# The output projection, norm and first factors of token block 2 moved ahead of the last three chunks of token block 1's MLP

## The chip, the core and the metric

The kernel runs on one core of a Trainium2 chip. The metric is the device time of one execution in microseconds (us). PE (TensorE) multiplies matrices, DVE (VectorE) and ACT (ScalarE) work elementwise, POOL (GpSimd) and SP (SyncE) issue DMAs. Each engine works through its own instructions in the order in which they are written for it.

## The reference

It is one layer of an encoder on x with 2048 tokens of 1024 numbers, all in float32:

```python
h = rms_norm(x)                               # x (1, 2048, 1024)
z = h @ w_in                                  # q, k, v of 8 + 4 heads, gate
mix = concat(neighbourhood_attention(8 heads), bidirectional_retention(4 heads) * silu(gate))
y = x + mix @ w_out                           # "out projection"
h2 = rms_norm(y)
y = y + square(relu(h2 @ w_up)) @ w_down      # 1024 -> 4096 -> 1024
out = rms_norm(y)
```

## The kernel before, in words

Every float32 operand is split into a high and a low part, and a product is three matmuls, high x high, high x low and low x high (lines 191, 192, 193). The weights are streamed: SP loads a raw piece (L169), ACT rounds it to its high part `wh` (L181), DVE subtracts to get the low part `wl` (L182). The raw pieces have two buffers, the split ones four.

The tokens are four blocks of 512. Blocks 0 and 1 go through their MLP as plain products in `mlp(j)`. Its 4096 hidden columns are eight pieces; "u" is a piece of the up product with its squared ReLU and "d" a piece of the down product, which adds to y. A u chunk is 96 matmuls in eight steps. A d chunk is too, in two halves of the columns with 48 matmuls each. "o" is the output projection of one block, 192 matmuls in sixteen steps, in two halves as well. A table, WORK, lists the chunks of each block in order. Blocks 2 and 3 have their MLP done together afterwards, by a scheme with seven products of sums of quarters ("the last phase", from about 1800 us). It reads its first factors from the DRAM tensor d_s.

A chain `main` yields 512 steps: 0 to 191 input projection, 192 to 207 output projection of block 0, 208 to 351 `mlp(0)`, 352 to 511 `mlp(1)`. `interleave` runs other generators beside it, each given a number of its own steps and the first and last step of `main` between which they are spread. So attention, `na(j)`, and retention, `ret(j)`, of one block run beside the MLP of an earlier one. PE's order is the order in which this is written. The other engines' orders come from a scheduler that goes by priority; once set, they too are worked through in order.

The steps that the change moves:

- `mix_load(j)`: loads the attention's output of block j (SP, L1032, into the two raw buffers of the weight stream) and splits it on ACT and DVE (L1033, L1034).
- `out_proj(j)`, "o2" and "o3": matmuls whose evictions on DVE add the residual x (L1055), which SP loads into tiles `st` (L1044); POOL stores the sum to d_y (L1056); ACT sums its squares (L1022).
- `norm_in(j)`: for four tiles of 128 rows, SP loads the row tile from d_y into one of two `xn` buffers (L1088), DVE scales it (L1089), PE transposes it in two groups of four (`hp`, L1071), DVE scales by the gain (L1073), and POOL stores to d_hT (L1075).
- `prep_first_half`: eight "puts". SP loads a piece of d_hT into an `st` tile (L1112), ACT casts it (L1106), DVE subtracts (L1107), and SP stores the pair `so` into d_s (L1108). The tiles `so` are two in all, used alternately.
- `finish_block(0)`: the final norm of block 0 and its store (L1011, L1012).
- `lend`: gives the tiles of retention to the pool of `st`. `gain_halves`: a small preparation of the gain.

The squared ReLU of a u chunk is L951 to L954 (ACT, DVE, ACT, DVE), where L952 frees the PSUM bank and L954 writes the last piece that d reads. The eviction of a d chunk is L991 on DVE. Products of four PSUM banks run together, three matmuls to a bank in turn. There are five banks with the tag `mm`, so a group starts with one free bank and needs the others from the evictions of the group before. The line numbers before and after are the same up to the table, and one higher after it.

Of the kernel before, what the change touches and what calls it, by code (L numbers as in the profile page):

```python
# [77 lines left out]
def trunk(ctx: ExitStack, tc: tile.TileContext, x, xT, w_in, w_out, w_up, w_down, g_mix, g_mixT, g_mlp, g_mlpT, g_fin, g_ret,  # L78
# [35 lines left out]
    def nm(s):  # L114
        uid[0] += 1
        return f"{s}_{uid[0]}"

    def newton(v, n):

        yi = cp.tile([P, 4], I32, tag="nwi", bufs=2, name=nm("nwi"))[:, :n]  # L120
        dve.tensor_scalar(out=yi, in0=v.bitcast(I32), scalar1=-0.5, scalar2=-554214945.0, op0=ALU.mult, op1=ALU.add)
        y = cp.tile([P, 4], F32, tag="nwy", bufs=4, name=nm("nwy"))[:, :n]
        t = cp.tile([P, 4], F32, tag="nwt", bufs=2, name=nm("nwt"))[:, :n]
        cur = yi.bitcast(F32)
        for _ in range(3):
            if n == 1:
                dve.scalar_tensor_tensor(out=t, in0=cur, scalar=v, in1=cur, op0=ALU.mult, op1=ALU.mult)
            else:
                dve.tensor_tensor(out=t, in0=cur, in1=cur, op=ALU.mult)
                dve.tensor_tensor(out=t, in0=t, in1=v, op=ALU.mult)  # L130
            dve.scalar_tensor_tensor(out=y, in0=t, scalar=-1.5, in1=cur, op0=ALU.add, op1=ALU.mult)
            cur = y
        return y

    def half_stat(v, ss, rest=EPS / 2):

        if isinstance(rest, float):
            dve.tensor_scalar(out=v, in0=ss, scalar1=0.5 / D, scalar2=rest, op0=ALU.mult, op1=ALU.add)
        else:
            dve.scalar_tensor_tensor(out=v, in0=ss, scalar=0.5 / D, in1=rest, op0=ALU.mult, op1=ALU.add)  # L140
        return v

    def stat_tile(n):
        return cp.tile([P, 4], F32, tag="nwv", bufs=2, name=nm("nwv"))[:, :n]
# [90 lines left out]
    gml = {}  # L235
# [60 lines left out]
    def transpose_split(xn, t, hT):  # L296
        for q in range(2):
            ps = ax.tile([P, 4, P], F32, tag="ax", name=nm("hp"))
            for i in range(4):
                pe.transpose(ps[:, i], xn[:, (q * 4 + i) * P:(q * 4 + i + 1) * P], ident)  # L300
            hi, lo = hT
            sl = (slice(None), slice(q * 4, q * 4 + 4), slice(t * P, (t + 1) * P))
            act.copy(out=hi[sl], in_=ps)
            dve.tensor_sub(out=lo[sl], in0=ps, in1=hi[sl].bitcast(F32))

    def big_tile(i, dtype, shape):
        return big.tile(shape, dtype, tag=f"big{i}", name=nm(f"big{i}"))

    def pair(i):
        return (big_tile(2 * i, F32R, [P, KT, GT]), big_tile(2 * i + 1, F32R, [P, KT, GT]))  # L310

    def xtile():
        return cp.tile([P, D], F32, tag="xn", bufs=2, name=nm("xn"))
# [566 lines left out]
    def norm_rows(g):  # L880
        ss = cp.tile([P, 4], F32, tag="ss4", bufs=2, name=nm("ss"))
        for t in range(4):
            jk = xtile()
            act.activation(out=jk, in_=g.y[:, t], func=AF.Square, accum_out=ss[:, t:t + 1])
        return rms_stat(ss, 4)

    def norm_block(g, gain):
        r = norm_rows(g)
        xs = {}

        def scaled(t):
            if t < 4:
                xs[t] = xtile()
                dve.scalar_tensor_tensor(out=xs[t], in0=g.y[:, t], scalar=r[:, t:t + 1], in1=gain, op0=ALU.mult,
                                         op1=ALU.mult)

        yield
        scaled(0)
        scaled(1)
        yield  # L900
        yield
        g.hT = pair(0)
        for t in range(4):
            transpose_split(xs[t], t, g.hT)
            scaled(t + 2)
            yield
# [96 lines left out]
    def finish_block(g):  # L1003
        r = norm_rows(g)
        yield
        gf = xtile()
        sp.dma_start(out=gf, in_=g_fin)
        yield
        for t in range(4):
            yt = g.y[:, t]  # L1010
            dve.scalar_tensor_tensor(out=yt, in0=yt, scalar=r[:, t:t + 1], in1=gf, op0=ALU.mult, op1=ALU.mult)  # L1011
            st_dma.dma_start(out=out[g.j * GT + t * P:g.j * GT + (t + 1) * P, :], in_=yt)  # L1012
            yield
# [10 lines left out]
    def mix_load(j, mix):  # L1024

        for q in range(4):
            if q % 2 == 0:
                mix.append(big_tile(3 - q // 2, F32R, [P, 4, 2, GT]))
            m = mix[-1]
            ks = slice(2 * (q % 2), 2 * (q % 2) + 2)  # L1030
            t = wp.tile([P, 2, 512], F32, tag="raw", bufs=RAW, name=nm("mraw"))
            sp.dma_start(out=t, in_=d_mix[q * 256:(q + 1) * 256, j * GT:(j + 1) * GT].rearrange("(k p) t -> p k t", p=P))  # L1032
            act.copy(out=m[:, ks, 0], in_=t)  # L1033
            dve.tensor_sub(out=m[:, ks, 1], in0=t, in1=m[:, ks, 0].bitcast(F32))  # L1034
            yield
# [30 lines left out]
    def norm_tile(j, t, rows, new):  # L1066

        for q in range(2):
            ps = ax.tile([P, 4, P], F32, tag="ax", name=nm("hp"))
            for i in range(4):  # L1070
                pe.transpose(ps[:, i], rows[:, (q * 4 + i) * P:(q * 4 + i + 1) * P], ident)  # L1071
            e = new([P, 4, P])
            dve.tensor_tensor(out=e, in0=ps, in1=gmlpT[:, q * 4:q * 4 + 4].unsqueeze(2).to_broadcast([P, 4, P]),  # L1073
                              op=ALU.mult)
            st_dma.dma_start(out=d_hT[q * 512:q * 512 + 512, (j - 2) * GT + t * P:(j - 2) * GT + (t + 1) * P]  # L1075
                         .rearrange("(i p) t -> p i t", p=P), in_=e)

    def norm_in(j):

        h = half_stat(stat_tile(4), ssums[j, 0])  # L1080
        r = cp.tile([P, 4], F32, tag="rs4", bufs=4, name=nm("rs"))
        dve.tensor_copy(r, newton(half_stat(stat_tile(4), ssums[j, 1], h), 4))
        ys = {}

        def scaled(t):
            if t < 4:
                ys[t] = xtile()
                sp.dma_start(out=ys[t], in_=d_y[j * GT + t * P:j * GT + (t + 1) * P, :])  # L1088
                dve.tensor_scalar(out=ys[t], in0=ys[t], scalar1=r[:, t:t + 1], scalar2=None, op0=ALU.mult)  # L1089

        scaled(0)
        scaled(1)
        yield
        for t in range(4):
            norm_tile(j, t, ys[t], st)
            scaled(t + 2)
            yield
# [73 lines left out]
    for kind, _ in CHUNKS:  # L1171
        for q in range(4):
            ws.add(w_in, q * 256, COL[kind])
    WORK = [("u", 0)]
    for b in range(1, 7):
        WORK += [("u", b), ("d", b - 1)]
    WORK = [WORK + [("d", 6)] + outs + [("u", 7), ("d", 7)] for outs in ([("o", 1)], [("o", 2), ("o", 3)])]

    def add_out(j):
        idx["o", j] = len(ws.aps)  # L1180
# [5 lines left out]
    for j in range(2):  # L1186
        for kind, b in WORK[j]:
            if kind == "o":
# [326 lines left out]
    def late(fn):  # L1515
        yield from fn()

    with tc.manual_schedule(engines={mybir.EngineType.PE}):
# [33 lines left out]
        def lend(tags):  # L1552
            lent.extend("r_" + t for t in tags)
            yield

        def mlp(j):
            for kind, b in WORK[j]:
                if kind == "o" and b == 1:
                    yield from out_block(groups[1], idx["o", 1])
                elif kind == "o":  # L1560
                    yield from out_proj(b, mixes[b], idx["o", b])
                elif kind == "u":
                    yield from mlp_up(groups[j], b, idx["u", j, b])
                else:
                    yield from mlp_down(groups[j], b, idx["d", j, b])
# [5 lines left out]
        def unlend(tags):  # L1571
            for t in tags:
# [3 lines left out]
        groups = [Group(j) for j in range(2)]  # L1576
        mixes = {2: [], 3: []}
        main = chain(project(hTs, before), late(lambda: first_out_proj(groups[0], idx["o", 0], gml[0])),
                     late(lambda: mlp(0)), late(lambda: mlp(1)))
        ALL = ("qk", "v", "g", "st", "qx", "kT", "qxT", "a")  # L1580
# [9 lines left out]
                (late(lambda: mix_block(groups[0])), 4, 183, 190),  # L1590
                (na(1), NA_STEPS, 182, 270), (ret(1), RET_STEPS, 190, 262),
                (late(lambda: y_load(groups[1])), 1, 303, 303), (late(lambda: mix_block(groups[1])), 4, 311, 316),
                (late(lambda: norm_block(groups[1], gml[0])), 7, 337, 351), (late(lambda: finish_block(groups[0])), 6, 430, 450),
                (na(2), NA_STEPS, 271, 360), (ret(2), RET_STEPS, 263, 330),
                (na(3), NA_STEPS, 361, 452), (ret(3), RET_STEPS, 368, 430),
                (late(lambda: lend(ALL)), 1, 453, 453),
                (mix_load(2, mixes[2]), 4, 455, 460), (mix_load(3, mixes[3]), 4, 473, 479),
                (late(lambda: norm_in(2)), 5, 484, 490), (late(prep_first_half), 4, 491, 497),
                (late(lambda: norm_in(3)), 5, 500, 507), (late(gain_halves), 1, 500, 500)]
        interleave(main, fill)  # L1600
        first.close()

# [102 lines left out]
```

## Time and profile before

| | |
|---|---|
| runs, us | 2435.49, 2440.76, 2434.04; median 2435.49 |
| the profiled execution, us | 2439.59 |
| its span, us | 2437.8 |
| PE busy in the span | 2352.9 us, 97%, 11000 matmuls |
| DVE, ACT, POOL busy | 1543.8 (63%), 951.7 (39%), 242.8 (10%) us |
| DMA | 433.89 MB, mean 178 GB/s |
| granted TensorE clock, mean | 0.983 of full speed |

All views are of one profiled execution. Times of the trace count from the span's start. Busy time is the time in which an engine executes; the idle time before an instruction is set down to what released it last. An idle engine that is not the bottleneck costs nothing.

### The profile page before, as it was taken

Reading aid. Unit: us, or ns where it says so; the run is one execution under the profiler, and the core shown is the slowest. Engines: PE = TensorE matmul, PEld = TensorE weight load, DVE = VectorE, ACT = ScalarE, POOL = GpSimd, SP = SyncE. Lnnn points to the kernel's source line nnn. Section 1 sums busy time; section 2 is a strip of 40 time slices with the busy share of each in tenths; the row PEclk is TensorE's granted clock in tenths of the full one; section 3 lists DMA queues with packets and bytes.
Section 4 is the critical chain, followed back from the end, with each engine's and each line's share of the span. In section 5 each row is a group of like instructions: output and inputs, shape, how many; then the busy total and the mean of one; then the engine's idle time right before and its main releaser. Section 6 shows DMA issues by size and latency. Waiting matters only on the chain.

```text
span 2437.8 us, 31360 instructions
## 1 busy us (share of the span) xinstructions
PE 2352.9 (97%) x11000; PEld 1910.5 (78%) x11000; DVE 1543.8 (63%) x2996; ACT 951.7 (39%) x1656; POOL 242.8 (10%) x351
## 2 busy tenths in 40 slices
PE   7999999899999999999999999999889999999997
PEld 6788888677778777777877777878768888888885
DVE  7326364445467666667666667664569859668598
ACT  5313233222334334333444333333346436353364
POOL 1213022221100000000000000000110210000012
PEclk9999999999999999999999999999989999999999
DMA  8545565866656655556644555536887462443511
GB/s 274 184 139 174 169 210 185 260 217 188 200 159 169 168 158 147 158 169 186 171 124 146 152 150 169 172 123 223 289 316 292 147 241 96 173 173 104 215 61 70
DMA packets 238205, 433.89 MB, mean 178 GB/s; under 512 B 29792, under 2 KB 102112, under 8 KB 233824
## 3 DMA queue, kind: packets, MB, share of 16 engines
q1 hardware_dynamic: 200704, 291.07, 39.1%
q0 software_dynamic: 26512, 115.38, 13.3%
q10 hardware_dynamic: 10832, 25.44, 4.0%
q8 instruction: 88, 1.44, 0.2%
q14 instruction: 69, 0.57, 0.1%
HBM read 343.69 MB, written 88.08 MB: 177 GB/s over the span
## 4 chain that ended last, share of the span: by engine, by line
issue 32%; PE 30%; DVE 6%; POOL 2%; ACT 1%; DMA 1%; POOLq 0%; SPq 0%; DVEq 0%; ACTq 0%
PE mm L1250 5%; PE mm L1248 5%; PE mm L1249 5%; PE mm L191 4%; PE mm L193 4%; PE mm L192 4%; DVE narrow L1266 1%; DVE wide L1271 1%; DVE ff L1297 1%; PE tp L644 1%; PE op L661 1%; DVE y L1405 1%; PE sp L612 1%; POOL d_hT L1075 0%; POOL d_y L1056 0%
## 5 line engine op out<-in xcount | busy, mean ns | idle before, releaser
L191 PE MATMUL mm<-wh,big 128*128 128x512 f32 (+1 forms) x1272 | 506.2, 398 | 19.4 <-DVE st L427 8.7
L193 PE MATMUL mm<-wh,big 128*128 128x512 f32 (+1 forms) x1272 | 491.8, 387 | 3.5 <-DVE big L954 3.5
L192 PE MATMUL mm<-wl,big 128*128 128x512 f32 (+1 forms) x1272 | 489.6, 385 | 0.8 <-DVE wl L182 0.8
L1250 PE MATMUL mm<-wide,narrow 128*128 128x512 f32 x896 | 350.3, 391 | 6.5 <-DVE narrow L1266 6.5
L181 ACT CAST wh<-raw 128x1024 fp32r<-128x1024 f32 x208 | 218.2, 1049 | 353.4 <-PE mm L193 165.3
L1248 PE MATMUL mm<-wide,narrow 128*128 128x512 f32 x896 | 349.8, 390 | 3.8 <-ACT narrow L1265 3.2
L191 PE MATMUL mm<-big,wh 128*128 128x512 f32 (+1 forms) x864 | 345.1, 399 | 7.9 <-DVE st L1055 3.5
L1249 PE MATMUL mm<-wide,narrow 128*128 128x512 f32 x896 | 349.6, 390 | 0.0
L182 DVE TENSOR_TENSOR wl<-raw,wh 128x1024 fp32r<-128x1024 f32 x206 | 254.7, 1236 | 141.6 <-ACT wh L181 139.6
L193 PE MATMUL mm<-big,wl 128*128 128x512 f32 (+1 forms) x864 | 333.2, 386 | 0.0
L192 PE MATMUL mm<-big,wh 128*128 128x512 f32 (+1 forms) x864 | 332.4, 385 | 0.0
L191 PEld LDWEIGHTS mm<-wh,big 128*128 128x128 f32 x1272 | 243.8, 192 | 76.8 <-issue 11.1
L193 PEld LDWEIGHTS mm<-wh,big 128*128 128x128 f32 x1272 | 243.1, 191 | 52.5 <-DVE big L954 3.9
L192 PEld LDWEIGHTS mm<-wl,big 128*128 128x128 f32 x1272 | 244.1, 192 | 42.1 <-DVE wl L182 1.1
L1250 PEld LDWEIGHTS mm<-wide,narrow 128*128 128x128 f32 x896 | 168.8, 188 | 43.6 <-DVE narrow L1266 8.7
L191 PEld LDWEIGHTS mm<-big,wh 128*128 128x128 f32 x864 | 163.7, 189 | 46.8 <-issue 12.2
L1248 PEld LDWEIGHTS mm<-wide,narrow 128*128 128x128 f32 x896 | 168.9, 188 | 39.9 <-ACT narrow L1265 4.1
L1249 PEld LDWEIGHTS mm<-wide,narrow 128*128 128x128 f32 x896 | 168.7, 188 | 35.3
L620 ACT ACTIVATE ns<-ns,nsc 128x288 f32<-128x288 f32 (+3 forms) x128 | 79.2, 619 | 283.7 <-DVE nsc L615 184.7
L193 PEld LDWEIGHTS mm<-big,wl 128*128 128x128 f32 x864 | 163.3, 189 | 33.5
L192 PEld LDWEIGHTS mm<-big,wh 128*128 128x128 f32 x864 | 163.8, 190 | 26.4
L662 DVE TENSOR_REDUCE nt<-op 128x128 f32<-128x256 f32 x128 | 53.8, 421 | 145.0 <-PE op L661 144.7
(251 smaller groups left out, 2978.7 us busy)
## 6 DMA issues: line engine op xcount, KB each, us to landing
wide<-d_s POOLq DMA_DIRECT2D x21, 2048.0 KB, 8.2
raw<-in_w_up_dram SPq DMA_DIRECT2D x64, 512.0 KB
raw<-in_w_down_dram SPq DMA_DIRECT2D x64, 512.0 KB
raw<-in_w_in_dram SPq DMA_DIRECT2D x48, 512.0 KB
raw<-in_w_out_dram SPq DMA_DIRECT2D x32, 512.0 KB
wq<-in_w_up_dram SPq DMA_DIRECT2D x16, 1024.0 KB
wq<-in_w_down_dram SPq DMA_DIRECT2D x16, 1024.0 KB
nv<-d_v SPq DMA_DIRECT2D x288, 36.0 KB
```

The source lines that it names most:

```text
L181: act.copy(out=hi, in_=t)
L182: (eng or dve).tensor_sub(out=lo, in0=t, in1=hi.bitcast(F32))
L191: pe.matmul(bank, lhsT=sh, rhs=mh, start=first, stop=False)
L192: pe.matmul(bank, lhsT=sh, rhs=ml, start=False, stop=False)
L193: pe.matmul(bank, lhsT=sl, rhs=mh, start=False, stop=last)
L612: pe.matmul(s_ps, lhsT=ql[lo_, qs], rhs=k3[lo_, 0:rows, band:band + w], start=False, stop=True)
L620: act.activation(out=s, in_=s, func=AF.Exp, bias=sc[:, 0:1], scale=-1.0, accum_out=sc[:, 2:3])
L644: pe.transpose(t_ps[:, g], s[:, g * kk:(g + 1) * kk], ident)
L662: dve.tensor_reduce(out=t2[:, c], in_=o_ps.rearrange("p s q -> p q s"), axis=mybir.AxisListType.X, op=ALU.add)
L1248: pe.matmul(banks[m], lhsT=sh, rhs=mh, start=first_, stop=False, skip_group_check=True)
L1249: pe.matmul(banks[m], lhsT=sh, rhs=ml, start=False, stop=False, skip_group_check=True)
L1250: pe.matmul(banks[m], lhsT=sl, rhs=mh, start=False, stop=last_, skip_group_check=True)
```

## The change

The table of block 1 gets an order of its own: u0, u1, d0, u2, d1, u3, d2, u4, d3, then d4, o2, u5, u6, d5, d6, o3, u7, d7. Before, it was ..., d3, u5, d4, u6, d5, d6, o2, o3, u7, d7. The mix loads, the norm and the first factors of block 2, the loan of retention's tiles, the small preparation of the gain and the end of block 0 move to steps that suit. In steps of `main`: o2 goes from 464-479 to 432-447, norm_in(2) from 484-490 to 453-460, prep_first_half from 491-497 to 464-476, finish_block(0) from 430-450 to 370-390. o3, u7 and d7 keep their steps, 480 to 511.

```diff
@@ -1174,7 +1174,8 @@
     WORK = [("u", 0)]
     for b in range(1, 7):
         WORK += [("u", b), ("d", b - 1)]
-    WORK = [WORK + [("d", 6)] + outs + [("u", 7), ("d", 7)] for outs in ([("o", 1)], [("o", 2), ("o", 3)])]
+    early = WORK[:9] + [("d", 4), ("o", 2), ("u", 5), ("u", 6), ("d", 5), ("d", 6), ("o", 3), ("u", 7), ("d", 7)]
+    WORK = [WORK + [("d", 6), ("o", 1), ("u", 7), ("d", 7)], early]
 
     def add_out(j):
         idx["o", j] = len(ws.aps)
@@ -1590,13 +1591,13 @@
                 (late(lambda: mix_block(groups[0])), 4, 183, 190),
                 (na(1), NA_STEPS, 182, 270), (ret(1), RET_STEPS, 190, 262),
                 (late(lambda: y_load(groups[1])), 1, 303, 303), (late(lambda: mix_block(groups[1])), 4, 311, 316),
-                (late(lambda: norm_block(groups[1], gml[0])), 7, 337, 351), (late(lambda: finish_block(groups[0])), 6, 430, 450),
+                (late(lambda: norm_block(groups[1], gml[0])), 7, 337, 351), (late(lambda: finish_block(groups[0])), 6, 370, 390),
                 (na(2), NA_STEPS, 271, 360), (ret(2), RET_STEPS, 263, 330),
                 (na(3), NA_STEPS, 361, 452), (ret(3), RET_STEPS, 368, 430),
-                (late(lambda: lend(ALL)), 1, 453, 453),
-                (mix_load(2, mixes[2]), 4, 455, 460), (mix_load(3, mixes[3]), 4, 473, 479),
-                (late(lambda: norm_in(2)), 5, 484, 490), (late(prep_first_half), 4, 491, 497),
-                (late(lambda: norm_in(3)), 5, 500, 507), (late(gain_halves), 1, 500, 500)]
+                (late(lambda: lend(ALL)), 1, 431, 431),
+                (mix_load(2, mixes[2]), 4, 423, 430), (late(lambda: norm_in(2)), 5, 453, 460), (late(prep_first_half), 4, 464, 476),
+                (mix_load(3, mixes[3]), 4, 472, 479), (late(gain_halves), 1, 490, 490),
+                (late(lambda: norm_in(3)), 5, 500, 507)]
         interleave(main, fill)
         first.close()
 
```

The first place is DVE around the puts. Before, o3's evictions (L1055, adding to the residual) stand among the subtractions L1107 of the puts; L182 is the weight stream:

```order
L182 TENSOR_TENSOR wl_15527<-raw_15470,wh_15526 128x1024
L1107 TENSOR_TENSOR so_15502<-st_15500,so_15502 128x512
L1055 TENSOR_TENSOR st_15372<-mm_15380,st_15372 128x512
L1107 TENSOR_TENSOR so_15508<-st_15506,so_15508 128x512
L1055 TENSOR_TENSOR st_15374<-mm_15381,st_15374 128x512
L1055 TENSOR_TENSOR st_15376<-mm_15382,st_15376 128x512
L1055 TENSOR_TENSOR st_15378<-mm_15383,st_15378 128x512
```

After, the first two stand directly ahead of the squared ReLU of u6 (L952, L954):

```order
L182 TENSOR_TENSOR wl_14912<-raw_14863,wh_14911 128x1024
L1107 TENSOR_TENSOR so_14983<-st_14981,so_14983 128x512
L1107 TENSOR_TENSOR so_14989<-st_14987,so_14989 128x512
L952 TENSOR_TENSOR st_14930<-mm_14770,st_14930 128x512
L952 TENSOR_TENSOR st_14938<-mm_14771,st_14938 128x512
L954 TENSOR_TENSOR big_2894_14769<-st_14930,big_2894_14769 128x512
```

The third pair and the fourth stand around the evictions of d5 (L991):

```order
L991 TENSOR_TENSOR big_1858_9789<-mm_14967,big_1858_9789 128x512
L1107 TENSOR_TENSOR so_15105<-st_15103,so_15105 128x512
L991 TENSOR_TENSOR big_1858_9789<-mm_14968,big_1858_9789 128x512
L182 TENSOR_TENSOR wl_15042<-raw_15005,wh_15041 128x1024
L1107 TENSOR_TENSOR so_15111<-st_15109,so_15111 128x512
L1107 TENSOR_TENSOR so_15178<-st_15176,so_15178 128x512
L182 TENSOR_TENSOR wl_15088<-raw_15039,wh_15087 128x1024
L1107 TENSOR_TENSOR so_15184<-st_15182,so_15184 128x512
L991 TENSOR_TENSOR big_1858_9789<-mm_15057,big_1858_9789 128x512
```

The puts have moved from the evictions of o3 to those of u6 and d5.

The second place is SP's queue ahead of d7, the loads of norm_in(3). Before, stores of first factors stand between the loads `xn`:

```order
L1088 DMA xn_15697<-d_y 128x1024
L169 DMA raw_15660<-in_w_down_dram 128x2x512
L1108 DMA d_s_96<-so_15550 128x1024
L1108 DMA d_s_95<-so_15608 128x1024
L1088 DMA xn_15700<-d_y 128x1024
L1108 DMA d_s_96<-so_15614 128x1024
L169 DMA raw_15719<-in_w_down_dram 128x2x512
L1088 DMA xn_15741<-d_y 128x1024
```

After:

```order
L169 DMA raw_15599<-in_w_down_dram 128x2x512
L1088 DMA xn_15701<-d_y 128x1024
L169 DMA raw_15634<-in_w_down_dram 128x2x512
L1088 DMA xn_15704<-d_y 128x1024
L169 DMA raw_15664<-in_w_down_dram 128x2x512
L169 DMA raw_15719<-in_w_down_dram 128x2x512
L1088 DMA xn_15741<-d_y 128x1024
```

No store of a first factor is left among them.

## Rows read from the trace of the kernel before

**Rows 1.** Windows: start:end, length, each engine's busy time (instructions), PEclk, DMA share, GB/s

```profile
1110.00:1190.00 80.00, 79.92 (x381) 63.82 (x381) 53.33 (x112) 29.42 (x51) 2.63 (x4) 1.00 0.71 193
1231.00:1238.00 7.00, 7.00 (x21) 5.41 (x22) 3.27 (x6) 0.59 (x1) 0.00 (x0) 0.66 0.30 98
1440.00:1640.00 200.00, 199.29 (x930) 159.66 (x929) 129.40 (x268) 72.00 (x129) 7.16 (x12) 1.00 0.52 155
1640.00:1700.00 60.00, 58.17 (x256) 47.66 (x255) 30.79 (x44) 21.40 (x32) 4.37 (x8) 1.00 0.66 217
1720.00:1724.00 4.00, 4.00 (x13) 3.13 (x12) 2.43 (x5) 0.00 (x0) 2.65 (x4) 0.57 0.92 281
1742.00:1748.00 6.00, 5.67 (x14) 4.35 (x15) 4.53 (x7) 2.97 (x7) 2.19 (x4) 0.53 0.89 292
1760.00:1780.00 20.00, 15.74 (x70) 12.56 (x69) 13.37 (x20) 7.09 (x11) 3.53 (x4) 0.83 0.99 357
1773.00:1779.00 6.00, 5.99 (x19) 4.90 (x20) 6.00 (x10) 2.10 (x4) 1.01 (x1) 0.55 1.09 421
```

**Rows 2.** Waits of PE, 1636 to 1800: total us, times, longest us

```profile
PE mm L191 <- DVE st L1055: 5.7, 3, 3.5
PE mm L193 <- DVE big L954: 3.5, 1, 3.5
PE hp L1071 <- DVE st L1073: 1.0, 1, 1.0
PE mm L191 <- DVE big L991: 0.9, 1, 0.9
PE hp L1071 <- DVE xn L1089: 0.8, 1, 0.8
PE mm L191 <- ACT big L953: 0.8, 1, 0.8
```

**Rows 3.** Timeline, PE: start, length, line, tiles, count, [idle before <-releaser]

```profile
1230.99 1.01 PE L661 MATMUL op<-npt,nv 120*128 120x256 f32 x3 [4.80 <-DVE big L304]
...
1711.11 0.50 PE L191 MATMUL mm<-wh,big 128*128 128x512 f32 x1 [1.28 <-DVE st L1055]
...
1719.49 0.66 PE L1071 MATMUL hp<-ident,xn 128*128 128x128 f32 x4 [1.02 <-DVE st L1073]
...
1738.17 0.39 PE L192 MATMUL mm<-big,wh 128*128 128x512 f32 x1
1738.40 0.39 PE L193 MATMUL mm<-big,wl 128*128 128x512 f32 x1
1742.33 0.80 PE L191 MATMUL mm<-big,wh 128*128 128x512 f32 x1 [3.54 <-DVE st L1055]
```

**Rows 4.** Timeline, ACT, the first factors' casts

```profile
1731.59 0.62 ACT L1106 CAST so<-st 128x512 fp32r<-128x512 f32 x1 [3.23 <-DMA st<-d_hT]
1734.23 0.62 ACT L1106 CAST so<-st 128x512 fp32r<-128x512 f32 x1 [2.02 <-DMA st<-d_hT]
...
1740.33 0.62 ACT L1106 CAST so<-st 128x512 fp32r<-128x512 f32 x1 [4.53 <-DMA d_s<-so]
```

**Rows 5.** Timeline, DVE

```profile
1521.62 3.67 DVE L1011 SCALAR_TENSOR_TENSOR big<-big,nwy,xn 128x1024 f32<-128x1024 f32 x3
...
1694.20 0.75 DVE L1089 TENSOR_SCALAR xn<-xn,rs 128x1024 f32<-128x1024 f32 x1 [1.40 <-DMA xn<-d_y]
...
1740.98 0.69 DVE L1107 TENSOR_TENSOR so<-st,so 128x512 fp32r<-128x512 f32 x1 [3.92 <-ACT so L1106]
...
1771.01 0.75 DVE L1089 TENSOR_SCALAR xn<-xn,rs 128x1024 f32<-128x1024 f32 x1 [2.94 <-DMA xn<-d_y]
```

**Rows 6.** Timeline, SP's queue: issues of DMAs

```profile
1689.95 0.33 SPq L1088 DMA_DIRECT2D xn<-d_y  x1
...
1728.71 2.25 SPq L1112 DMA_DIRECT2D st<-d_hT  x5
...
1764.17 4.20 SPq L1088 DMA_DIRECT2D xn<-d_y  x2
```

## The prediction, made before the changed kernel ran

> **What bounds the kernel now.** The page comes first: PE, the TensorE matmul engine, is busy 97% of the span, so time is gained or lost only where PE stands still or runs at the lower clock. The change touches a stretch that ends at 1800 us, and a table of windows over it shows where PE is not full: attention with MLP chunks, 1440 to 1640, keeps it busy 199.29 of 200 us, while 1760 to 1780 reaches 15.74 of 20 at a granted clock of 0.83 [rows 1]. The list of PE's waits, cut to 1636 to 1800, names them: 5.7 + 3.5 + 1.0 + 0.9 + 0.8 + 0.8 = 12.7 us [rows 2]. The timeline places the large ones. Output projection o3 pauses between its halves (1.28) and around the last transposes of norm_in(2) (0.8, 1.02), and the first matmul of u7 waits 3.54 for an eviction of o3 [rows 2, 3]. The 3.5 on L954 is the first matmuls of d7, waiting for u7's squared ReLU.
>
> After the larger ones the clock falls from 2.4 to about 1.2 GHz. A window's length times what its granted clock lacks of 1 gives the cost: 4 x 0.43 = 1.7 after the transposes, 6 x 0.47 = 2.8 after the 3.54, 6 x 0.45 = 2.7 after the 3.51 [rows 1]. Idle time and clock together are 12.7 + 7.2 = 19.9 us, all that the change can win before 1800. What follows 1800 reads the same factors and is written in the same order, so I leave its waits alone.
>
> Two chains make the waits. The put of a first factor is a load of d_hT, a cast on ACT (L1106), a subtraction on DVE (L1107), and a store from one of two buffers. ACT stood 4.53 us for the stores d_s<-so of the first pair before it could cast again at 1740.33, and DVE stood 3.92 behind that cast [rows 4, 5]. DVE works in order, and o3's evictions (L1055) stand behind that subtraction: hence 3.54 on PE. At d7, DVE stands 2.94 us for a load xn<-d_y with u7's evictions behind it [rows 5].
>
> **The change, part by part.** Nothing is added or removed; every matmul, cast and DMA is issued once as before. What moves is o2, its mix loads, norm_in(2) with its two transposes per row tile and 4 stores, the 8 puts with 8 loads and 8 stores, and finish_block(0).
>
> What goes. Between o3's halves and at the transposes there is no norm_in(2) any more: 1.28 + 0.8 + 1.02 = 3.1, and the clock's 1.7: 4.8. At o3 to u7 no put stands among the evictions: 3.54 + 2.8 = 6.3. At u7 to d7 the load of xn is still ahead of the evictions on DVE, but eight d_s stores no longer share SP and the DMA engines with it. Issued at 1764.17, it let DVE start at 1771.01, 6.8 us later, at a DMA share of 0.99 [rows 1, 5, 6]. The like load issued at 1689.95 was used at 1694.20, 4.25 us later, at 0.66. So DVE is 2.6 us earlier; PE's 3.51 becomes 0.9, the 0.8 beside it stays, and I expect no fall of the clock after waits of that size (the 0.9 behind L991 and the 0.92 left of the 5.7 brought none; that stretch has a clock of 1.00 [rows 1, 2]). That saves 2.6 + 2.7 = 5.3. Bounds: nothing, if the load is no faster, and 6.7, if both waits shrink to 0.3. Together 4.8 + 6.3 + 5.3 = 16.4.
>
> A rule on this load, apart from that sum: the Trainium skill, "DMA: Bandwidth & Descriptors", section "Latency and other measured facts", gives an HBM access 0.2 us on average and 2 us at high load, and calls the fixed cost of a DMA smaller under lighter load. The trace agrees in sign, 6.8 against 4.25 us, but differs by 2.6 us and not by at most 1.8. By the page's figure, as an estimate, 0.8 us less would be won here, and the total would come out that much later.
>
> What comes back. (1) The puts now stand ahead of u6's squared ReLU: the first pair's cast on ACT and subtraction on DVE precede all four evictions. Before, the last transposes began at 1719.49 and ended 0.66 later, 1720.15; the first casts began at 1731.59 and 1734.23, 11.4 and 14.1 later, with the loads of d_hT issued at 1728.71, after the stores landed [rows 3, 4, 6]. In the new order 48 matmuls lie between those transposes and the end of u6, at 0.23 each [rows 3] 11.0 us, and d5 has one free PSUM bank, worth 3 matmuls or 0.7. If the second cast comes after 14.1, its subtraction and the first eviction (0.6 to 0.7 each) end at 16.1: PE waits 4.5. If it comes with the first cast, 11.4, the eviction ends by 13.4 and PE waits 1.7; with stores and loads each 0.5 faster than that, 0.7. I take 3.0, since the DMA share of that stretch should lie between 0.52 and 0.92 (attention's and the old place's [rows 1]); and 2.0 for the clock, between nothing and 2.8. Five together, 0.7 to 7.3.
>
> (2) d5 to d6. Puts stand among d5's evictions (L991) of one half and directly ahead of those of the other. With PE a whole half-chunk of matmuls (48, 11.0 us) behind each, the turnaround of a buffer pair, 1734.23 to 1740.33 or 6 us, mostly fits. I take 0.7, between nothing and 3.0 (the wait of 3.54 at u7, a little shorter).
>
> (3) o2 among attention. The mix loads and residual loads join the attention's loads on SP's queue, and PE is in order. The like combination ran in 1110 to 1190, the output projection of token block 1 beside na(2): 79.92 us busy of 80 [rows 1]. I take 0.5, between nothing and 3.0. What norm_in(2) costs there is in this too, as u5 and u6 run beside it.
>
> (4) o3 to u7 keeps an ordinary wait on an eviction like the others: 0.9 [rows 2]. finish_block(0), four DVE operations from 1521.62 [rows 5], goes from one attention stretch to another; it lay in 1440 to 1640, where PE lost 0.7 of 200, so nothing, at most 0.7. If attention's cover were gone, its four operations would cost 4 x 1.3 = 5 us of DVE.
>
> Sum: -16.4 + 5.0 + 0.7 + 0.5 + 0.9 = -9.3. The profiled execution took 2439.59, so 2430.3 in its place; it is 4.1 over the median of the runs, 2435.49, and a median should come to 2426.2.
>
> **Rivals.** (a) The puts' wait only changes its place. They are as long as before, and ACT and DVE still meet them in order ahead of evictions. Then u6 to d5 costs 7.3 and d5 to d6 the old 6.3: -9.3 + 2.3 + 5.6 = -1.4, 2434.1. For it: the same 4.53 for a store would stand ahead of L991. Against it: 11.0 us of matmuls in between.
>
> (b) The load of xn is no faster, because what it meets is the weight stream and the next phase's factors, which stay. u7 to d7 then keeps its 7.0: -9.3 + 5.3 = -4.0, 2431.5. For it: the 1.09 share of 1773 to 1779, when no put was left [rows 1]. Against it: the two stores issued shortly before.
>
> (c) Slower: SP's queue delays attention. A mix load waits for one of two weight buffers and a residual load for an st tile; loads of attention's values (nv) and of weights stand behind it. PE met a late attention product at 1230.99, idle 4.80, then 7 us at 0.66: 4.8 + 2.4 = 7.2 [rows 1, 3]. Two such waits leave +5.1, still within the noise; from the third it is slower: -9.3 + 21.6 = +12.3, 2447.8. For it: na(3) runs on through o2. Against it: 1110 to 1190.
>
> **How the numbers follow.** About 0.3%, 7.3 us, is what a measurement here can tell from no change: faster is under 2428.2, slower over 2442.8. The forecast has 0.60, with its own range from the best ends, -16.2 or 2419, to the worst of the sum's new terms, -4.7 or 2431; 0.50 of it is faster and 0.10 the same. A gain beyond 2419 has 0.04. Rival (a) has 0.14, all the same; (b) 0.11, of which 0.03 faster; (c) 0.11, slower. That makes 0.57, 0.32 and 0.11. The range from 2417 to 2438 holds the forecast, (a) and (b), and leaves out (c) and the largest gain.
>
> **What would show it.** In the profile after: no wait of PE between o3 and u7 above 1 us and no clock near 0.5 there; DVE's wait for xn before d7 well below 2.94; one new wait of 2 to 5 us at the start of d5, with ACT's casts L1106 released by st<-d_hT just before; no op L661 wait beside o2. I would be wrong if waits on L1055 or L991 of 3 us or more stand at d5 and d6 together, if d7's start still costs 3.5, or if PE has new waits on attention's products near o2.

## The result and the profile after

The changed kernel takes 2419.7 us (median of 4 runs, 2417.94 to 2423.2) against 2434.76 before: 15.1 us less, a ratio of 0.9933 with a 95% interval of 0.9921 to 0.9945. In five later rounds the ratio was 0.9932 (0.9913 to 0.9951). The forecast was faster, 2426.2 us in a range of 2417 to 2438. The time lies in the range and near its lower end: the gain is 1.6 times the 9.3 us that were worked out.

The page's span goes from 2437.8 to 2421.4 us. The windows after, to be held against [rows 1] (start:end, length, busy time of PE, PEld, DVE, ACT and POOL with their instructions, granted clock, DMA share, GB/s):

```profile
1440.00:1640.00 200.00, 199.31 (x946) 160.11 (x945) 128.19 (x269) 75.03 (x139) 15.76 (x24) 1.00 0.62 187
1640.00:1700.00 60.00, 58.22 (x255) 47.23 (x254) 36.31 (x47) 22.91 (x30) 0.00 (x0) 1.00 0.73 246
1700.00:1760.00 60.00, 60.00 (x276) 49.76 (x274) 29.17 (x45) 21.01 (x35) 5.87 (x10) 1.00 0.53 174
1760.00:1780.00 20.00, 18.39 (x89) 15.29 (x88) 8.18 (x14) 2.68 (x8) 7.15 (x10) 1.00 0.99 366
```

The clock is 1.00 in all of them, and the stretch after the puts, 1700 to 1760, has PE busy for 60.00 of 60 us at a DMA share of 0.53. The attention stretch with o2 and norm_in(2) in it, 1440 to 1640, loses 0.69 us, where it lost 0.71.

PE's waits up to the last phase, to be held against [rows 2]:

```profile
PE hp L1071 <- DVE st L1073: 1.6, 1, 1.6
PE mm L191 <- DVE st L952: 1.3, 2, 1.0
PE mm L191 <- DVE big L991: 0.5, 1, 0.5
```

They sum to 3.4 us, where they were 12.7. The timeline of PE gives their places (start, length, line, tiles, count, idle before), first the last transposes of norm_in(2) and the start of d5, then the transposes of norm_in(3) in d7 and the start of the last phase:

```profile
1631.76 1.04 PE L1071 MATMUL hp<-ident,xn 128*128 128x128 f32 x8
...
1645.36 0.50 PE L191 MATMUL mm<-wh,big 128*128 128x512 f32 x1 [0.99 <-DVE st L952]
...
1647.34 0.50 PE L191 MATMUL mm<-wh,big 128*128 128x512 f32 x1 [0.33 <-DVE st L952]
```

```profile
1761.74 0.66 PE L1071 MATMUL hp<-ident,xn 128*128 128x128 f32 x4 [1.61 <-DVE st L1073]
...
1784.40 0.50 PE L1249 MATMUL mm<-wide,narrow 128*128 128x512 f32 x1 [2.04 <-ACT narrow L1266]
```

The last phase began at 1801.01 before and begins at 1784.40, 16.6 us earlier. Idle time gives 12.7 - 3.4 = 9.3 of that, and the three half-clock stretches of [rows 1], all gone, give 7.2: 16.5. After that nothing has changed beyond 0.2 us.

Where the forecast put the new wait, at d5, 1.0 + 0.3 us stand without a fall of the clock. The casts of the first pair of puts on ACT, to be held against [rows 4]:

```profile
1639.50 0.62 ACT L1106 CAST so<-st 128x512 fp32r<-128x512 f32 x1 [0.35 <-DMA st<-d_hT]
1643.36 0.62 ACT L1106 CAST so<-st 128x512 fp32r<-128x512 f32 x1 [3.23 <-DMA st<-d_hT]
...
1656.41 0.62 ACT L1106 CAST so<-st 128x512 fp32r<-128x512 f32 x1 [4.28 <-DMA d_s<-so]
```

They come 6.7 and 10.6 us after the end of the transposes (1632.80), not 11.4 and 14.1. DVE's row at 1644.01, the subtraction of the second put, still stands directly ahead of the first evictions of u6, and the second row is the scaling of the third row tile ahead of d7, which waits for its load of xn, to be held against [rows 5]:

```profile
1644.01 0.69 DVE L1107 TENSOR_TENSOR so<-st,so 128x512 fp32r<-128x512 f32 x1 [2.99 <-ACT so L1106]
...
1754.22 0.75 DVE L1089 TENSOR_SCALAR xn<-xn,rs 128x1024 f32<-128x1024 f32 x1 [1.59 <-DMA xn<-d_y]
```

SP's issues of these loads, as [rows 6]:

```profile
1636.37 4.31 SPq L1112 DMA_DIRECT2D st<-d_hT  x6
...
1750.64 6.68 SPq L1088 DMA_DIRECT2D xn<-d_y  x2
```

The first load of d_hT goes out 3.6 us after the transposes, where it was 8.6; from its issue to the cast it takes 3.1 us, where it took 2.9. So the whole difference lies ahead of the load, and POOL's stores to d_hT show where, before and after:

```profile
1721.35 2.99 POOL L1075 DMA_DIRECT2D d_hT<-st  x4 [6.85 <-DVE st L1073]
```

```profile
1633.39 0.75 POOL L1075 DMA_DIRECT2D d_hT<-st  x1 [1.49 <-DVE st L1073]
1635.11 0.75 POOL L1075 DMA_DIRECT2D d_hT<-st  x1 [0.97 <-DVE st L1073]
```

After, the last two, of the fourth row tile, leave singly at 1633.39 and 1635.11, 0.6 and 2.3 us after the end of the transposes. Before, four of them left one behind the other from 1721.35, since DVE had stood 3.50 us for a load of xn (its scaling at 1716.95) with the evictions of two row tiles behind it. The first load of d_hT is issued when the first store of the fourth row tile has landed (1728.57 and 1728.71 before, 1636.31 and 1636.37 after). That store left 2.7 us after the transposes before and leaves 0.6 after; from its leaving to the load's issue it took 5.9 us and takes 3.0. The 5.0 us are thus 2.1 from DVE and POOL and 2.9 from the landing. That the new place is quieter does not show in the DMA share over the chain itself, before and after:

```profile
1720.00:1730.00 10.00, 10.00 (x39) 8.07 (x38) 3.66 (x6) 1.05 (x1) 2.99 (x4) 0.83 0.75 246
```

```profile
1636.00:1644.00 8.00, 8.00 (x37) 6.58 (x36) 1.83 (x2) 2.32 (x4) 0.00 (x0) 1.00 0.88 281
```

Over 1632 to 1636, as the last stores leave, it is 0.70. Further ahead the new place is the quieter one: 0.82 over 1620 to 1632, where it was 0.95 over 1705 to 1720.

The load of xn issued at 1750.64 is used at 1754.22, 3.6 us later, where it was 6.8. It also goes out earlier. Its buffer comes free when the first row tile of norm_in(3) has been transposed. These are those transposes before, with SP's last store of a first factor, and the transposes after:

```profile
1760.60 1.04 PE L1071 MATMUL hp<-ident,xn 128*128 128x128 f32 x8
```

```profile
1763.26 0.32 SPq L1108 DMA_DIRECT2D d_s<-so  x1
```

```profile
1749.57 1.04 PE L1071 MATMUL hp<-ident,xn 128*128 128x128 f32 x8
```

Before, the load (1764.17) stood in SP's order behind that store, which waited for the last put's subtraction, and went out 2.5 us after the buffer was free (1761.64). After, it goes out at once (1750.61 to 1750.64). From the free buffer to the scaling it is 3.6 us instead of 9.4.

### The profile page after: what moved, and what is told of

Read it like the earlier page. It is cut to its first block, busy times and chain, and to the rows that moved or that the text cites. A ratio compares the mean times of both kernels' runs of the same rounds, so it can differ in the third digit from the quotient of the medians.

```text
span 2421.4 us, 31361 instructions
## 1 busy us (share of the span) xinstructions
PE 2345.3 (97%) x11000; PEld 1906.1 (79%) x11000; DVE 1543.3 (64%) x2996; ACT 951.5 (39%) x1656; POOL 243.5 (10%) x351
## 4 chain that ended last, share of the span: by engine, by line
PE 36%; issue 26%; DVE 5%; DMA 1%; POOL 1%; ACT 1%; POOLq 0%; SPq 0%; DVEq 0%; ACTq 0%
PE mm L1251 6%; PE mm L1249 6%; PE mm L1250 6%; PE mm L191 5%; PE mm L193 5%; PE mm L192 5%; DVE narrow L1267 1%; DVE ff L1298 1%; PE tp L644 1%; PE sp L612 1%; DVE y L1406 1%; DVE wide L1272 1%; PE op L661 1%; DMA d_s<-so 0%; PE sp L610 0%
## 5 line engine op out<-in xcount | busy, mean ns | idle before, releaser
L182 DVE TENSOR_TENSOR wl<-raw,wh 128x1024 fp32r<-128x1024 f32 x206 | 254.6, 1236 | 137.0 <-ACT wh L181 134.5
```

The lines of the kernel that those rows point to most:

```text
L182: (eng or dve).tensor_sub(out=lo, in0=t, in1=hi.bitcast(F32))
```

## The experiments

Ratios are those to the kernel before on the same chip, with 95% intervals. Waits are of one profiled execution each. Single traces of one kernel differ by some us in parts that the change does not touch, so the ratio tells the time and the trace only the place. after_again came out as expected: 15.1 us under the kernel before, waits of 0.8 + 0.3 us at d5 and 1.7 at the transposes of norm_in(3), nothing ahead of u7.

| kernel | what is different | median us | ratio |
|---|---|---|---|
| after_again | nothing, the changed kernel | 2420.9 | 0.9932 (0.9913 to 0.9951) |
| puts_late | after, puts back | 2425.9 | 0.9944 (0.9926 to 0.9962) |
| norm_puts_late | after, norm_in(2) and puts back | 2432.3 | 0.9972 (0.9962 to 0.9982) |
| end0_late | after, end of block 0 back | 2420.1 | 0.9926 (0.9906 to 0.9945) |
| copies_norm2 | after, copies ahead of the puts | 2424.9 | 0.9954 (0.9936 to 0.9972) |
| copies_d7 | after, copies ahead of d7 | 2424.2 | 0.9940 (0.9922 to 0.9957) |
| so_five | before, five buffers so | 2438.7 | 1.0014 (1.0002 to 1.0026) |
| xn_behind | before, scaling of xn later | 2436.8 | 1.0003 (0.9992 to 1.0015) |
| norm2_480 | before, norm_in(2) four steps earlier | 2436.1 | 0.9994 (0.9984 to 1.0005) |
| norm2_early | after, puts four steps later | 2419.1 | 0.9937 (0.9919 to 0.9954) |
| norm2_449 | after, norm_in(2) four steps earlier | 2423.1 | 0.9937 (0.9922 to 0.9953) |
| norm2_norm3 | after, puts and norm_in(3) later | 2427.4 | 0.9963 (0.9950 to 0.9976) |

**The parts of the change undone.** First the puts alone:

```diff
-(late(prep_first_half), 4, 464, 476)
+(late(prep_first_half), 4, 491, 497)
```

> The changed kernel with prep_first_half alone back at steps 491 to 497. Theory: the waits at o3 to u7 and at u7 to d7 both came from the puts, so both return: about 3.5 us on L1055 ahead of u7 with a half-clock stretch, and 3 to 4 us on L954 or L953 ahead of d7 with another, the load xn<-d_y taking 6 to 7 us; the 1.3 + 0.5 at d5 and d6 goes. 2428 to 2433 us. Rival: the load of xn was slow because of norm_in(3)'s own order and not because of the puts: then only the wait ahead of u7 returns, 2424 to 2426 us.

PE's waits from 1636 to the last phase:

```profile
PE hp L1071 <- DVE st L1073: 1.7, 1, 1.7
PE mm L191 <- DVE st L1055: 0.9, 2, 0.6
```

Both theories miss. (The median lies in the rival's range, but the wait that the rival names is not there.) DVE's order is again a subtraction, an eviction of o3, a subtraction and three evictions, but the wait ahead of u7 is 0.9 us and nothing waits ahead of d7. What differs from the kernel before is that d_hT has been complete for long. Casts on ACT ahead of and among o3's evictions (the first row is two):

```profile
1722.74 1.37 ACT L1106 CAST so<-st 128x512 fp32r<-128x512 f32 x2 [3.00 <-DMA st<-d_hT]
...
1729.19 0.62 ACT L1106 CAST so<-st 128x512 fp32r<-128x512 f32 x1 [0.62 <-DMA d_s<-so]
```

The first put of all was cast at 1650.35; five follow from 1713.64 to 1729.19, around the evictions, and the last two at 1739.75 and 1740.77, in u7. The place of the puts in the queues of ACT and DVE is therefore not by itself what cost 3.54 us before. The third load of norm_in(3) goes out as soon as its buffer is free here too, at 1747.35. The ratio, 0.9944 against 0.9932, is not told from the changed kernel's, as the intervals overlap. In this trace the last phase begins at 1781.40; it then waits 3.4 us for its first factors.

Then norm_in(2) as well:

```diff
-(late(lambda: norm_in(2)), 5, 453, 460), (late(prep_first_half), 4, 464, 476)
+(late(lambda: norm_in(2)), 5, 484, 490), (late(prep_first_half), 4, 491, 497)
```

> The changed kernel with norm_in(2) back at 484 to 490 and prep_first_half at 491 to 497; only o2, its mix loads, the loan and the end of block 0 stay moved. Theory: o2's place by itself earns next to nothing and all of the old waits return (between o3's halves, at the transposes, ahead of u7 and d7): 2433 to 2437 us. Rival: o2 among attention earns by itself, since its boundaries with d and u chunks then cost nothing: 2429 to 2432 us.

PE's waits from 1636 to 1800:

```profile
PE mm L193 <- DVE big L954: 4.0, 1, 4.0
PE hp L1071 <- DVE xn L1089: 2.0, 2, 1.6
PE mm L191 <- DVE st L1055: 1.9, 2, 1.7
PE mm L191 <- ACT big L953: 1.8, 1, 1.8
PE hp L1071 <- DVE st L1073: 1.0, 1, 1.0
```

Now the transposes wait again (2.0 + 1.0), and d7 waits 1.8 + 4.0: the third load of norm_in(3) stands behind a put's store on SP once more (issued at 1764.06, used at 1771.42). Ahead of u7 only 1.9 are left. The time is 0.28% under the kernel before, some 7 us, which is the size of the rival's: o2 among attention earns by itself. The boundaries of o2 that cost 0.9 each in [rows 2], d6 to o2 and o2 to o3, and the 1.28 between o3's halves are gone in this trace, but with the waits that grew the list sums to 10.7 us, only 2.0 under 12.7. The rest is mostly clock: no half-clock stretch stands behind the shorter wait ahead of u7.

The two kernels in a row say what each part is worth: 7 us for o2, about as much for norm_in(2) (0.9972 to 0.9944), and what is left, 0.9944 to 0.9932, for the puts, which the intervals do not tell from nothing. The traces put the parts in the same order. From the end of retention's last product (L787) to the start of the last phase, 1204 matmuls in each kernel, PE takes:

| | before | norm_puts_late | puts_late | changed | after_again |
|---|---|---|---|---|---|
| us | 285.2 | 280.1 | 267.0 | 268.2 | 268.2 |

So o2 earns 5.1 us, norm_in(2) 13.1 less the 3.4 that puts_late pays in the last phase, and the puts earn only by not paying those. This stretch, too, is of one execution: in xn_behind, below, it is 5.3 us shorter than before, with no gain in the median.

The end of block 0 alone, at its old steps:

```diff
-(late(lambda: finish_block(groups[0])), 6, 370, 390)
+(late(lambda: finish_block(groups[0])), 6, 430, 450)
```

> The changed kernel with finish_block(0) back at 430 to 450, beside o2. Theory: nothing hangs on it, 2418 to 2422 us, no new wait of PE over 1 us between 1500 and 1660. Rival: its four DVE operations of 1.3 us delay o2's evictions or attention: a PE wait of 2 us or more near o2 and 2423 us or more.

The theory holds: 0.9926, and the only wait over 1 us in that window is the known one at d5, 1.4 + 0.3 us in all.

**Traffic.** Copies from d_y to a DRAM tensor that nothing reads, which wait for the rows that o2 (below: o3) has stored:

```diff
+def copies():
+    for i in range(8):
+        sp.dma_start(out=d_copy[i], in_=d_y[2 * GT + i % 4 * P:2 * GT + (i % 4 + 1) * P, :])
+        yield
...
+(late(copies), 8, 454, 463)
```

> The changed kernel with eight extra copies of 512 KB from DRAM to DRAM on SP's queue at steps 454 to 463, ahead of the loads of d_hT for the puts; they add work that nothing needs. Theory: the puts reached u6's end in time because the DMA engines were less busy, so with this traffic the first two casts come 11 to 14 us after the last transposes instead of 6.7 and 10.6, and PE waits 3 to 5 us on L952 at d5, with a half-clock stretch: 2424 to 2428 us. Rival: they were in time because DVE and POOL evicted and stored each transpose at once, and traffic does not matter: L952 wait under 2 us, 2419 to 2422 us.

The last transposes and the start of d5 on PE, and the first pair's casts on ACT:

```profile
1630.25 1.04 PE L1072 MATMUL hp<-ident,xn 128*128 128x128 f32 x8
...
1646.41 0.50 PE L192 MATMUL mm<-wh,big 128*128 128x512 f32 x1 [3.56 <-DVE st L953]
...
1648.40 0.79 PE L192 MATMUL mm<-wh,big 128*128 128x512 f32 x1 [0.23 <-DVE st L953]
```

```profile
1639.69 0.62 ACT L1107 CAST so<-st 128x512 fp32r<-128x512 f32 x1 [2.05 <-DMA st<-d_hT]
1644.42 0.62 ACT L1107 CAST so<-st 128x512 fp32r<-128x512 f32 x1 [4.10 <-DMA st<-d_hT]
```

The casts come 8.4 and 13.1 us after the end of the transposes (1631.29), 1.7 and 2.5 later than in the changed kernel; the first is earlier than the theory's 11. DVE and POOL are as quick as there: the store leaves 0.6 us after the transposes. But from then to the first load it is 5.0 us instead of 3.0. PE waits 3.6 + 0.2 us at d5, the forecast's kind and size, and the matmul at 1648.40 (0.79 us) is at the lower clock. So d5 has nothing to spare: the 2.5 us by which the second cast comes later are the 2.5 by which PE waits longer. The ratio lies 0.2% over the changed kernel's, with overlapping intervals.

The same copies, from block 3's rows, at steps 498 to 503:

> The changed kernel with eight extra copies of 512 KB from DRAM to DRAM on SP's queue, spread over steps 498 to 503 among the loads of norm_in(3); they add work that nothing needs. Theory: the traffic beside the load of xn made it slow, so it takes 5.5 us or more again and PE waits 2.5 to 4 us ahead of d7, with a half-clock stretch: 2424 to 2428 us. Rival: traffic does not matter there, the load takes 3.6 us as in the changed kernel, 2418 to 2421 us.

DVE's scaling of row tiles of norm_in(3), and SP's issues of their loads:

```profile
1755.23 0.75 DVE L1090 TENSOR_SCALAR xn<-xn,rs 128x1024 f32<-128x1024 f32 x1 [2.85 <-DMA xn<-d_y]
...
1763.17 0.75 DVE L1090 TENSOR_SCALAR xn<-xn,rs 128x1024 f32<-128x1024 f32 x1 [0.50 <-DMA xn<-d_y]
```

```profile
1747.95 1.04 SPq L1089 DMA_DIRECT2D xn<-d_y  x2
...
1757.22 0.33 SPq L1089 DMA_DIRECT2D xn<-d_y  x1
```

The first load takes 7.3 us (1747.95 to 1755.23) where it takes 5.0 in the changed kernel (1734.91 to 1739.91), and the third 5.9 (1757.22 to 1763.17) instead of 3.6: copies beside a load do slow it. As they are issued on SP's queue as well, it is open whether it is the traffic or the place behind them in that queue. PE waits only 0.5 + 0.6 us ahead of d7, since the scheduler, which counts the copies too, puts the scaling behind two evictions of u7 here. Half the theory is shown, the load's time; that its delay alone costs 3 us on PE is not. (The median lies in the theory's range, but the larger new waits of this trace, 1.62 us at 1630.15 and 1.94 at 1650.69 with a fall of the clock, stand ahead of the copies.)

**The kernel before with one wait taken away.** Five buffers for the pairs so, from tiles that attention has left:

```diff
-o = np_.tile([P, 2, 512], F32R, tag=("n_k", "n_pt")[turn2[0] % 2], bufs=1, name=nm("so"))
+w = turn2[0] % 5
+if w > 1:
+    tags = (("n_qh", 1), ("n_ql", 1)) if w == 2 else ((("n_s", "n_v")[w - 3], 2),) * 2
+    o = [np_.tile([P, 512], F32R, tag=t, bufs=n, name=nm("so")) for t, n in tags]
...
+    for c in range(2):
+        sp.dma_start(out=d_s[i][:, kk, c], in_=o[c].bitcast(F32))
+    return
+o = np_.tile([P, 2, 512], F32R, tag=("n_k", "n_pt")[w], bufs=1, name=nm("so"))
```

> The kernel before with five buffers for the first factors' pairs (so) in place of two, the three new ones taken from tiles that attention has left by then; each of those pairs is stored in two halves. Theory: the 3.5 us ahead of u7 came from the casts' wait for stores of so, so it falls under 1.2 us and its half-clock stretch goes; the waits at the transposes and ahead of d7 stay: 2428 to 2431 us. Rival: the loads of d_hT are as late as the stores, so the wait ahead of u7 stays above 2.5 us: 2433 to 2436 us.

The longest of PE's waits from 1636 to 1800:

```profile
PE hp L1071 <- DVE xn L1089: 6.4, 1, 6.4
PE mm L191 <- DVE st L1055: 6.1, 3, 2.5
...
```

The wait ahead of u7 falls from 3.5 to 2.5 only, and the clock still falls after it (0.72 over 1743 to 1749). The first cast now comes 12.6 us after the transposes, waiting 6.0 for the load of d_hT, and the transposes of norm_in(3) wait 6.4 for their load, with all eight puts' stores ahead of it on SP. No time is won. Neither theory is right alone.

The scaling of the third and fourth row tile put behind u7's evictions (the scaling moves into the loop for all four tiles, with one step more ahead of the third; norm_in(2) has the same code):

```diff
-dve.tensor_scalar(out=ys[t], in0=ys[t], scalar1=r[:, t:t + 1], scalar2=None, op0=ALU.mult)
...
 for t in range(4):
+    if t == 2:
+        yield
+    dve.tensor_scalar(out=ys[t], in0=ys[t], scalar1=r[:, t:t + 1], scalar2=None, op0=ALU.mult)
     norm_tile(j, t, ys[t], st)
```

> The kernel before, with the scaling of the third and fourth row tiles in norm_in (and their transposes) placed a step later, so that on DVE the wait for the third load xn<-d_y stands behind u7's squared ReLU and not inside it; loads and stores stay. Theory: the 0.8 + 3.5 us ahead of d7 and their half-clock stretch came from DVE's order behind that late load, so they fall under 1.5 us in all even with the puts' stores where they were: 2429 to 2432 us against 2436. Rival: the late load's transposes then stop PE in d7 itself, with a wait on xn of 3 us or more: 2434 to 2438 us.

PE's timeline at the start of u7 and at the transposes ahead of d7:

```profile
1734.73 0.50 PE L191 MATMUL mm<-big,wh 128*128 128x512 f32 x1 [2.70 <-DVE st L1055]
...
1737.15 0.80 PE L191 MATMUL mm<-big,wh 128*128 128x512 f32 x1 [1.47 <-DVE st L1055]
...
1763.16 1.06 PE L1071 MATMUL hp<-ident,xn 128*128 128x128 f32 x8 [2.80 <-DVE xn L1096]
```

The wait on L954 is gone, but transposes stand 2.80 us for xn, and u7's start has 2.70 + 1.47. The rival holds: the time does not change. (The span of this trace, 2429.0, is 8 us under the median of its runs; it is the fastest of the twelve.)

norm_in(2) four steps earlier in the old order:

```diff
-(late(lambda: norm_in(2)), 5, 484, 490)
+(late(lambda: norm_in(2)), 5, 480, 486)
```

> The kernel before, with norm_in(2) four steps earlier, 480 to 486, and nothing else moved: 48 more matmuls lie between its last transposes and the end of o3, and the puts still stand among o3's evictions. Theory: the wait ahead of u7 came from d_hT landing late and not from the puts' place, so it falls from 3.5 to under 1.5 us without its half-clock stretch, and the stores of the puts end earlier, so that the wait ahead of d7 shrinks too: 2426 to 2431 us against 2436. Rival: the puts wait for so's stores wherever they stand, and the 3.5 us stays: 2434 to 2438 us.

The longest of PE's waits from 1636 to 1798:

```profile
PE mm L191 <- DVE st L1055: 6.9, 2, 5.3
PE hp L1071 <- DVE xn L1089: 4.7, 1, 4.7
...
```

The theory fails where it was most certain. Ahead of u7 PE waits 5.3 us. d_hT is complete earlier, and so the scheduler puts six casts ahead of o3's evictions, and ACT's third and sixth wait for stores of so:

```profile
1734.49 0.62 ACT L1106 CAST so<-st 128x512 fp32r<-128x512 f32 x1 [5.62 <-DMA d_s<-so]
...
1745.24 0.62 ACT L1106 CAST so<-st 128x512 fp32r<-128x512 f32 x1 [4.58 <-DMA d_s<-so]
```

Ahead of d7 the wait on L954 is gone, as expected, but the transposes of norm_in(2) wait 4.7 for a load that was issued at 1690.89 and used at 1695.68, right behind o2. So three single cures each move the wait to its neighbour: what is short between the end of o2 and d7 is time for the whole chain.

**Other placings of the new order.**

```diff
-(late(prep_first_half), 4, 464, 476)
+(late(prep_first_half), 4, 468, 478)
```

> The changed kernel with norm_in(2) four steps earlier, 449 to 456, so that 96 matmuls lie between its last transposes and the end of u6 instead of 48. Theory: the first two pairs are done before u6's squared ReLU, and the waits at d5 (1.0 + 0.3 us) go: 2417 to 2420 us. Rival: the second pair, now ahead of u6's squared ReLU as well, waits for stores of so and the wait at d5 grows to 2 us or more: 2421 to 2425 us.

The kernel that ran under this name had the edit shown and not the one that the expectation speaks of: norm_in(2) stayed where the change has it. So the expectation does not apply to it. It ran like the changed kernel (0.9937), with 1.1 + 0.3 us at d5. The edit that was meant:

```diff
-(late(lambda: norm_in(2)), 5, 453, 460)
+(late(lambda: norm_in(2)), 5, 449, 456)
```

> The changed kernel with norm_in(2) at 449 to 456 and prep_first_half left at 464 to 476; 96 matmuls lie between the last transposes of norm_in(2) and the end of u6 instead of 48, and four casts of puts stand ahead of u6's squared ReLU instead of two. (In the run norm2_early it was prep_first_half that moved, to 468 to 478, and norm_in(2) stayed.) Theory: a pair of casts takes about 6 us, two pairs fit into the 22 us, and the waits at d5 stay at 1.5 us or less: 2417 to 2421 us. Rival: four casts ahead of the evictions are one pair too many, as six were ahead of u7 in norm2_480, and PE waits 3 us or more at d5: 2424 to 2428 us.

PE's waits from 1560 to 1782:

```profile
PE mm L191 <- DVE st L952: 1.8, 2, 1.5
PE hp L1071 <- DVE st L1073: 1.7, 1, 1.7
...
```

The wait at d5 is 1.8 us, and the time that of the changed kernel within the intervals. Two pairs fit into the 22 us of a chunk; the third pair of norm2_480 was too many.

The start of the last phase, with norm_in(3) later as well:

```diff
-(late(prep_first_half), 4, 464, 476)
+(late(prep_first_half), 4, 468, 478)
-(late(lambda: norm_in(3)), 5, 500, 507)
+(late(lambda: norm_in(3)), 5, 502, 508)
```

> The changed kernel with prep_first_half at 468 to 478 and norm_in(3) at 502 to 508. Theory: the transposes of norm_in(3) no longer meet u7's squared ReLU on DVE, so the 1.6 us on hp goes, and the rest stays: 2417 to 2419.5 us. Rival: the transposes and stores come too late for the last phase, whose start then waits longer: 2421 us or more.

PE's waits at the start of the last phase:

```profile
PE mm L1249 <- ACT narrow L1266: 6.6, 3, 3.4
PE mm L1251 <- DVE narrow L1267: 4.3, 4, 1.7
```

They sum to 10.9 us from 1784 to 1900, against 5.9 in the changed kernel: the first steps of the last phase get late factors. The transposes of norm_in(3) still wait 1.4. The rival holds: 0.9963. No placing that was tried beats the change.

## Why the prediction was right, and where it was not

The bound, the places of the old waits and their price were right: 19.9 us were said to be all that could be won, and 16.5 of them were. The direction followed. The size did not: 16.5 is just over the best end of the sum, 16.2, so all the misses point one way, and the new wait of 2 to 5 us at d5 that was to show the mechanism did not come.

The 4.8 us between o3's halves and at its transposes went as forecast. norm_puts_late ties the transposes' part to norm_in(2): put back beside o3, it brings their waits back. It does not bring back the 1.28 between o3's halves, so norm_in(2) beside o3 is not enough to cause that wait.

The 6.3 us ahead of u7 went. The reason given, that no put stands among the evictions, is not the whole of it: puts_late puts them there and pays 0.9. norm2_480 and so_five show the rest of the cause: the puts' turns of about 6 us for a pair and the loads of d_hT have to end before the evictions behind them. Before, three subtractions of puts stood ahead of the evictions of o3's second half, and the third needed a buffer back (the 4.53 of [rows 4]); in the new order two stand ahead of u6's.

The 5.3 us ahead of d7 came out nearly in full: 1.6 us are left, where 1.7 was said, but on the transposes and not on the evictions, so that the agreement is chance. The prediction counted from the load's issue and had DVE 2.6 us earlier. It left out SP's wait ahead of the issue: 2.5 us there and 3.3 in the load make 5.8, which takes the whole of that wait. puts_late and norm_puts_late show it: with the puts' stores done early the load goes out at once and nothing waits, with a late one ahead of it d7 waits 1.8 + 4.0. The load takes 3.6 us, less than the 4.25 that were taken. The 4.25 were read beside a DMA share of 0.66, which is that of a window of 60 us; over the load itself, 1689.95 to 1694.20, the share is 0.92, and in puts_late a load at 0.97 takes 3.8. So the share alone does not tell a load's time. copies_d7 shows that copies ahead of it slow it, and xn_behind that the wait on L954 came from the place of the scaling in DVE's order; that the d_s stores alone had made the load slow is not shown.

The estimate from the Trainium skill, "DMA: Bandwidth & Descriptors", section "Latency and other measured facts", was that 0.8 us less would be won here, as its two latencies of an HBM access, 0.2 and 2 us, lie 1.8 apart. The trace does not agree: the load's time fell by 3.3 us.

The step that failed in size is (1), u6 to d5: 5.0 us were set, 1.3 were measured, 3.7 of the 7.2 us by which the sum was off. Its arithmetic was right and its input was not. With the second cast 10.6 us after the transposes in place of 14.1, its own working gives 10.6 + 2.0 - 11.0 - 0.7 = 0.9, and 0.99 was measured; with the 13.1 of copies_norm2 it gives 3.4, and 3.56 was measured. The 11.4 and 14.1 came from a place where DVE stood 3.50 us for a load and POOL's last four stores left in a row and landed late; over the chain itself the DMA share is no lower in the new place (0.88 against 0.75), only ahead of it (0.82 against 0.95). copies_norm2 shows that traffic can make the landing 2.0 us longer; what made it 2.9 longer in the old place, and what the earlier evictions are worth alone, was not varied. (In norm2_449 the distance is 11.4 again, without any wait of 3 us: what the distance costs depends on the matmuls that lie over it.)

The second miss is that boundaries that cost 0.9 each were left in the sum, d6 to o2 and o2 to o3, and a third was added in (4). After, none of them waits: 2.7 us. norm_puts_late, in which o2 alone stays moved, has no wait at its old two either. Why an eviction beside attention comes in time was not tried.

Steps (2) and (3) came out at 0.5 and 0 for 0.7 and 0.5. These four differences, 0.1 at d7, 3.7, 2.7 and 0.7, are the 7.2 us between -9.3 and -16.5 in the trace.

Of the rivals, (a) is excluded by the waits at d5 and d6, (b) by the load's 3.6 us, and (c) by the window 1440 to 1640. (a) was real all the same: in copies_norm2 PE waits 3.8 us at d5, of the 4.5 in its price, with a fall of the clock.

## What to carry to other kernels

A round trip through DRAM that an in-order engine must end before it may evict needs as much matmul time over it as all its links and turns take together. Where such a chain is squeezed between two stages, curing one wait (more buffers, another order, an earlier start) hands it to the next, as in three kernels here; moving the whole chain to where fewer of its turns stand ahead of an eviction gave time to every link. A duration read in one place holds that place's queues. Take it apart (leaving, landing, issue, load) before it enters a sum for another place, and look for the wait ahead of an issue as well as the time behind it.

## What was not expected of the hardware

How much of the gain is clock: 7.2 of the 16.5 us. In the changed kernel the granted clock is 1.00 through its waits of up to 1.6 us before the last phase; in so_five a wait of 2.48 us was followed by 0.72 over 1743 to 1749, and in norm2_480 one of 5.28 by 0.77 over 1747 to 1754. The length of one wait does not tell it: before, the stretch at 0.57 from 1720 stood behind two waits of only 0.8 and 1.02 us, with four transposes between them [rows 1, 2, 3]. After the change the waits that had such a stretch behind them are gone, and the stretches with them.
